# Feed-forward input products as seven products of quarters, with the inner features in slabs

## The chip, the cores and the metric

One core of one Trainium2 chip runs the whole program in one launch. The metric is device microseconds of an execution. A core has a matrix engine (TensorE, "PE" in the profile) whose weight loads are listed apart ("PEld"), and VectorE (DVE), ScalarE (ACT) and GpSimd (POOL), each of which works through its own instructions in program order. SyncE (SP) issues most DMAs. Matmuls write to PSUM, which here is used as two pairs of banks and four single banks.

## The reference, cut to what matters

Two layers act on 528 tokens (16 learned ones ahead of 512) of 1024 features, in float32. Each has a feed-forward block, a token mixer (layer 0 differential attention, layer 1 gated linear attention) and a second feed-forward block:

```python
def rmsnorm(x, g):
    y = x * lax.rsqrt(jnp.mean(x * x, axis=-1, keepdims=True) + RMS_EPS)
    return y * g

def swiglu(h, w_in, w_out):            # w_in 1024 x 5632, w_out 2816 x 1024
    gu = h @ w_in
    g, u = gu[..., :D_FF], gu[..., D_FF:]
    return (jax.nn.silu(g) * u) @ w_out

for i in range(2):
    h = h + 0.5 * swiglu(rmsnorm(h, ffn1_norm[i]), ffn1_w_in[i], ffn1_w_out[i])
    h = h + mixer_i(rmsnorm(h, mix_norm[i]))
    h = h + 0.5 * swiglu(rmsnorm(h, ffn2_norm[i]), ffn2_w_in[i], ffn2_w_out[i])
return rmsnorm(h, final_norm)[:, 16:]
```

The four feed-forward blocks are called a, b (layer 0) and c, d (layer 1) here and in tile names: `ps_bi` is PSUM of b's input products, `ps_bo` of its output products. Block d needs only the last 512 tokens.

## The kernel before, in words

The residual `xr` lies in SBUF, features on partitions, as eight tiles of 128 x 528. Each float32 product is done in three passes over two exact parts of each operand, high (`h`) and low (`l`): wh*xh, wh*xl, wl*xh (`linear`, L230). ScalarE casts the high part of a chunk of weights (`split_chunk`, L190), VectorE or GpSimd subtracts it for the low part (L191); a chunk is 128 x 1024 and there are three rooms for chunks (raw, high and low). Chunks come in one list (`plan`) in order of use, and each `take` loads and splits those behind it.

The norm's gain goes into the activations' parts (`split_x`, L283 on ScalarE, L284 on VectorE); 1/rms (`rms_scale`) multiplies what comes out. It comes from a sum of squares that GpSimd adds up tile by tile (`add_square`, L296 and L300), a product with ones (L339) and a chain on ScalarE and VectorE (L305 to L312).

A feed-forward block (`ffn`) first runs 44 input products, g and u for each of 22 inner features of 128 rows. Each takes eight blocks of the contraction, three passes, two halves of the tokens of 264 columns into two banks (in d one pass of 512 columns into one bank). `done` scales by 1/rms, applies silu and multiplies (L457 to L466); the parts of all 22 hidden features stay in SBUF. Then `project_out` runs eight output products of 22 blocks each; behind each, VectorE adds to the residual (L369) and the parts and the square for the next norm are made. The next stage starts on seven eighths of its first contraction before it needs the last block. At the very start three products run side by side while pieces of x and of the weights come in. `finish` does the last output block by halves of the tokens, so that one half's final norm runs under the other half's matmuls.

Everything is in program order (`manual_schedule`); the mixers place their steps by slots and ranks (`timeline`), with projections as filler, and the first three blocks of their output products begin under the last head (`finish_all`).

## Time and profile before

| | |
|---|---|
| median of 3 runs | 2118.15 us (2115.76 to 2120.3) |
| span of the profiled execution (its own time is given by this) | 2114.5 us |
| TensorE matmuls busy | 2062.8 us, 98% |
| VectorE, ScalarE, GpSimd busy | 1080.8, 739.8, 259.1 us |
| input products of b, without its first contraction | 743.78 to 993.34 us |
| output products of b | 993.34 to 1120.64 us |
| HBM read | 174.26 MB, 83 GB/s |

Times are counted from the first instruction. Matmuls are pipelined, so the duration of one (285 ns for 264 columns) is longer than the distance from one start to the next. The chain of waits is followed back from the last instruction to what released each step.

### The profile page before, as it was taken

To read this page: it belongs to the slowest core of one execution; us is meant where nothing else is said; L and a number is where in the kernel's file an instruction comes from. 1 tells how busy PE (TensorE), PEld (TensorE's weight loads), DVE (VectorE), ACT (ScalarE), POOL (GpSimd) and SP (SyncE) were. 2 spreads that over 40 slices of the span, in tenths; PEclk is the share of its full clock that TensorE was granted. 3 is DMA by queue.
4 is the path that set the end of the run, shared out by engine and by line. 5 is a ranking of instruction groups with operands and counts; after the bars stand their busy time and mean duration, and the time that the engine had idled before them with its cause. 6 is when DMAs were issued, how large, how long until landed. Compare 5 with 4: busy or idle time off the path is not lost.

```text
span 2114.5 us, 34232 instructions
## 1 busy us (share of the span) xinstructions
PE 2062.8 (98%) x14654; PEld 1920.3 (91%) x14654; DVE 1080.8 (51%) x1653; ACT 739.8 (35%) x1224; POOL 259.1 (12%) x193
## 2 busy tenths in 40 slices
PE   8999999999899999999999999999999999999998
PEld 8999999977777999999999999999988878888886
DVE  6444433488888654444334444433366665444333
ACT  5222222355555432222223222222544452222223
POOL 2000000334331200000000000000333220000001
PEclk9999999999999999999999999999999999999999
DMA  4233233211110223233322223233222222332332
GB/s 156 96 90 91 88 93 90 81 51 40 42 49 31 81 90 91 90 91 95 90 86 97 95 90 91 88 93 90 81 71 70 71 90 90 100 96 94 92 97 71
DMA packets 52586, 178.57 MB, mean 84 GB/s; under 512 B 5825, under 2 KB 8002, under 8 KB 52434
## 3 DMA queue, kind: packets, MB, share of 16 engines
q1 hardware_dynamic: 52112, 176.25, 27.2%
q8 instruction: 115, 1.88, 0.4%
q14 instruction: 37, 0.30, 0.0%
q10 hardware_dynamic: 322, 0.13, 0.0%
HBM read 174.26 MB, written 2.10 MB: 83 GB/s over the span
## 4 chain that ended last, share of the span: by engine, by line
PE 88%; DVE 8%; ACT 2%; issue 1%; DMA 0%; POOL 0%; SPq 0%; DVEq 0%; ACTq 0%; POOLq 0%
PE ps_bi L230 12%; PE ps_ci L230 12%; PE ps_ai L230 12%; PE ps_di L230 11%; PE ps_co L230 6%; PE ps_ao L230 6%; PE ps_bo L230 6%; PE ps_do L230 5%; PE ps_dak L230 2%; PE ps_dao L230 2%; PE ps_glao L230 2%; PE ps_gva L230 1%; PE ps_s L642 1%; PE ps_gvb L230 1%; PE ps_gob L230 1%
## 5 line engine op out<-in xcount | busy, mean ns | idle before, releaser
L230 PE MATMUL ps_ai<-xh,wh_ai 128*128 128x264 f32 x704 | 144.2, 286 | 5.4 <-ACT xh L283 5.3
L230 PE MATMUL ps_ai<-xl,wh_ai 128*128 128x264 f32 x704 | 143.0, 284 | 1.1 <-DVE xl L284 1.0
L230 PE MATMUL ps_ci<-xh,wh_ci 128*128 128x264 f32 x704 | 143.1, 285 | 0.0
L230 PE MATMUL ps_bi<-xh,wh_bi 128*128 128x264 f32 x704 | 143.1, 285 | 0.0
L230 PE MATMUL ps_ai<-xh,wl_ai 128*128 128x264 f32 x704 | 142.1, 284 | 0.5 <-DVE wl_ai L191 0.5
L230 PE MATMUL ps_bi<-xl,wh_bi 128*128 128x264 f32 x704 | 141.9, 283 | 0.0
L230 PE MATMUL ps_ci<-xl,wh_ci 128*128 128x264 f32 x704 | 141.9, 283 | 0.0
L230 PE MATMUL ps_bi<-xh,wl_bi 128*128 128x264 f32 x704 | 141.3, 282 | 0.0
L230 PE MATMUL ps_ci<-xh,wl_ci 128*128 128x264 f32 x704 | 141.3, 282 | 0.0
L230 PE MATMUL ps_di<-xh,wl_di 128*128 128x512 f32 x352 | 138.8, 394 | 0.0
L230 PE MATMUL ps_di<-xh,wh_di 128*128 128x512 f32 x352 | 138.7, 394 | 0.0
L230 PE MATMUL ps_di<-xl,wh_di 128*128 128x512 f32 x352 | 137.3, 390 | 0.0
L230 PEld LDWEIGHTS ps_ai<-xh,wh_ai 128*128 128x128 f32 x704 | 109.3, 189 | 5.8 <-ACT xh L283 5.3
L230 PEld LDWEIGHTS ps_ai<-xl,wh_ai 128*128 128x128 f32 x704 | 109.9, 189 | 1.8 <-DVE xl L284 1.8
L230 PEld LDWEIGHTS ps_ai<-xh,wl_ai 128*128 128x128 f32 x704 | 108.7, 188 | 1.0 <-DVE wl_ai L191 1.0
L230 PEld LDWEIGHTS ps_ci<-xl,wh_ci 128*128 128x128 f32 x704 | 109.2, 188 | 0.0
L230 PEld LDWEIGHTS ps_bi<-xl,wh_bi 128*128 128x128 f32 x704 | 109.2, 188 | 0.0
L230 PEld LDWEIGHTS ps_ci<-xh,wh_ci 128*128 128x128 f32 x704 | 108.7, 188 | 0.1
L230 PEld LDWEIGHTS ps_bi<-xh,wh_bi 128*128 128x128 f32 x704 | 108.7, 188 | 0.1
L230 PEld LDWEIGHTS ps_bi<-xh,wl_bi 128*128 128x128 f32 x704 | 108.2, 188 | 0.0
L230 PEld LDWEIGHTS ps_ci<-xh,wl_ci 128*128 128x128 f32 x704 | 108.2, 188 | 0.0
L673 ACT ACTIVATE e<-ps_s,nb,rq 64x264 f32<-64x264 f32 (+3 forms) x96 | 54.6, 570 | 83.6 <-DVE nb L662 53.9
(544 smaller groups left out, 5199.3 us busy)
## 6 DMA issues: line engine op xcount, KB each, us to landing
wraw_bi<-in_f_in SPq DMA_DIRECT2D x44, 512.0 KB, 3.6
wraw_ci<-in_f_in SPq DMA_DIRECT2D x44, 512.0 KB, 3.6
wraw_di<-in_f_in SPq DMA_DIRECT2D x44, 512.0 KB, 3.6
wraw_ai<-in_f_in SPq DMA_DIRECT2D x41, 512.0 KB, 3.6
wraw_ao<-in_f_out SPq DMA_DIRECT2D x16, 512.0 KB, 3.6
wraw_bo<-in_f_out SPq DMA_DIRECT2D x16, 512.0 KB, 3.5
wraw_co<-in_f_out SPq DMA_DIRECT2D x16, 512.0 KB, 3.5
wraw_do<-in_f_out SPq DMA_DIRECT2D x16, 512.0 KB, 3.5
```

Source lines behind the costliest of these rows:

```text
L230: nc.tensor.matmul(put(b, at, at + c1 - c0), w[:, ws], x[:, c0:c1], start=first, stop=last,)
L642: nc.tensor.matmul(o, qm[m][rows, qs], kl[rows, c0 : c0 + n], start=False, stop=True)
L673: act.activation(es_[t][m][: NQ[t], c0:c1], p, AF.Exp, bias=nb, scale=rq[: NQ[t], t : t + 1], accum_out=sm[:, i, m : m + 1],)
```

## The change

Write the 256 rows of g and u of an inner feature as two block rows, the contraction as two halves (even and odd tiles of 128 features) and the tokens as two halves. The product of a 2 x 2 and a 2 x 2 of quarters takes eight products of quarters; Strassen's method (in a form with shared sums) takes seven, P1 to P7, of sums and differences of quarters. P1 uses A11 and the first half of even x, P2 uses A12 and the first half of odd x; the others use s1 to s4 (weights, four sums a feature, on VectorE) and t1 to t4 (activations, four differences of each pair of tiles). The sums of the seven products go partly through PSUM: P1, P6, P5 and P3 add up in one bank, P7 and P4 in another, and what lies between is copied or added out (`evacuate`).

The seven products have 4 blocks of the contraction, three passes and one half of the tokens each. Inner features are taken in slabs of 2, 4, 4, 4, 4, 4; while the input products of a slab run, the output products of the slab before are put between them, each block of a slab adding to the residual by itself. Output weights come in pieces of up to 512 columns. The last slab's output products stand alone at the end of the block, with the sums for the next norm behind each. All stages share two SBUF areas (`ra`, `fa`) by fixed offsets. The loading order at the start changes, and the squares of x are now behind all sums (`head`).

Core of the diff (new code; the old `ffn`, `want_ffn` and `next_parts` go):

```diff
+SLABS = (2, 4, 4, 4, 4, 4)
+NQ = KD // 2
+AHEAD = 6
+NRING = 9
+    def plain(i, gcol, tok, k):
...
+        act.activation(h, x, AF.Copy, scale=g)
+        dve.scalar_tensor_tensor(l, x, g, h.bitcast(F32), op0=ALU.mult, op1=ALU.subtract)
+    def scaled(i, gcol, tok, k, z):
...
+        act.activation(z[:, 2 * k : 2 * k + 2, :n], tokens(xr[j], tok), AF.Copy, scale=...)
+        if k == 0:
+            dve.tensor_tensor(out=z[:, 4, :n], in0=z[:, 0, :n], in1=z[:, 1, :n], op=ALU.subtract)
+    def sums(i, tok, z, fine):          # t2, t3, t4 on DVE, then parts of t1..t4
...
+            out(3, 7)                   # act.copy of 4 x 264
+            rest(3, 7)                  # dve subtract of 4 x 264
+    def next_block(kind, gcol, acc, j, c0, z=None, last=False):
+        if kind == "parts":
+            split_x(j, gcol, c0)
+        elif kind == "seven":
+            plain(i, gcol, tok, k)
+        add_square(acc, j, c0)
+        if kind == "seven":
+            scaled(i, gcol, tok, k, z)
+            if k:
+                sums(i, tok, z, last and j == KD - 1)
...
+    def in_units():
+        order = [(0, "P1"), (1, "P1"), (0, "P2")]
+        order += [(0, p) for p in ("P6", "P7", "P5", "P3", "P4")] + [(1, "P2")]
+        for f in range(1, KF):
+            order += [(f, p) for p in ("P6", "P7", "P5")]
+            order += [(f + 1, "P1"), (f, "P3"), (f, "P4"), (f + 1, "P2")]
...
+    class in_stream:                    # tasks in order: s1, s2, s3, cut P6, s4, cut P7, ...
+        def step(self):                 # a sum on DVE, or a cast on ACT and a subtract on DVE
...
+            def evacuate(f, p):
+                if p == "P1":
+                    act.copy(g[:, 0], A)
+                elif p == "P2":
+                    dve.tensor_tensor(out=g[:, 0], in0=banks["B", f], in1=g[:, 0], op=ALU.add)
+                    if R:
+                        dve.tensor_tensor(out=g[:, 0], in0=g[:, 0], in1=r(0), op=ALU.mult)
+                elif p == "P6":
+                    act.copy(u[:, 0], A)
+                elif p == "P5":
+                    act.copy(u[:, 1], A)
+                    dve.tensor_tensor(out=u[:, 1], in0=banks["D", f], in1=u[:, 1], op=ALU.add)
+                elif p == "P3":
+                    dve.tensor_tensor(out=g[:, 1], in0=A, in1=r(1), op=ALU.mult)
...
+                    act.activation(g, g, AF.Silu)
+                elif p == "P4":
+                    dve.tensor_tensor(out=u[:, 0], in0=banks["D", f], in1=u[:, 0], op=ALU.add)
+                    dve.scalar_tensor_tensor(u, u, -1.0, r(), op0=ALU.mult, op1=ALU.mult)
...                                      # later: u *= g, its high part (ACT), its low part (DVE)
+            def product(f, p):
...
+                for i in range(NQ):
+                    for c, (w, v) in enumerate(((wh, xh), (wh, xl), (wl, xh))):
+                        nc.tensor.matmul(banks[k, f], w[:, ws], v, ...)
+            def bring(c, what):         # output weights: load, or cast, subtract and load c + 2
...
+            for i, u in enumerate(work):
+                if len(u) == 3:
+                    out_piece(*u)
+                else:
+                    product(*u)
...                                      # stream.step() up to AHEAD products on; late steps
+                    evacuate(*u)
+                    if u == (0, "P6"):
+                        R.append(rms_scale(acc, name, c0))
...
+            for j in range(KD):         # the last slab's output products
+                for c in range(pieces(tail)):
+                    out_piece(tail, j, c)      # piece 0 also brings the next weights
...
+                out_done(tail, j)              # add to the residual; next_block
+                if kind == "parts" and j in (5, 6):
+                    split_to(j - 5)
+                if kind == "seven" and j >= 4:
+                    nxt.to(2 * (j - 3))
...
+            if z == 0:                  # in finish, now over the last slab alone
+                table(LN_EXP)
...
+                if j == 5:              # behind the mixers' output blocks
+                    ahead.start()
+                    ahead.to(2)
+            ahead.to(6)
...
+    load_x(0, 2)
+    first.load(0, 0)
+    load_x(4, 6)
+    first.load(1, 0)
+    load_x(1, 3, 5, 7)
+    first.load(0, 1)
+    first.load(1, 1)
+    def head(z):
+        for i in range(KD // 2):
+            plain(i, V_F1[0], False, 0)
+            if i in (0, 3):
+                first.to(1 + i // 3)
+        for i in range(KD // 2):
+            plain(i, V_F1[0], False, 1)
+        first.to(3)
+        zs = [z, room_for_sums(fa[:, ZF : ZF + 8 * HALF])]
+        for i in range(KD // 2):
+            for k in range(2):
+                scaled(i, V_F1[0], False, k, zs[i % 2])
+            sums(i, False, zs[i % 2], False)
+        first.to(6)
+        for k in range(KD):
+            add_square(acc, k)
```

## Rows read from the trace of the kernel before

**Rows 1.** The page: busy time of each engine, and the granted clock in slices.
```profile
PE 2062.8 (98%) x14654; PEld 1920.3 (91%) x14654; DVE 1080.8 (51%) x1653; ACT 739.8 (35%) x1224; POOL 259.1 (12%) x193
...
PEclk9999999999999999999999999999999999999999
```
**Rows 2.** Chain that ended last: start us, us, engine, tile, line, count.
```profile
64.17 202.73 PE ps_ai L230 x1680
...
742.89 0.89 PE ps_ss_b L339 x4
743.78 249.55 PE ps_bi L230 x2070
993.34 127.31 PE ps_bo L230 x1056
...
1741.84 238.06 PE ps_di L230 x1035
...
2086.15 7.85 PE ps_last L402 x66
```
**Rows 3.** Window over the input products of b (columns: header line).
```profile
core 0: us, PE busy (x) PEld busy (x) DVE busy (x) ACT busy (x) POOL busy (x), PEclk, DMA share, GB/s
743.78:993.34 249.56, 249.56 (x2073) 249.56 (x2072) 116.09 (x136) 70.53 (x91) 0.00 (x0) 1.00 0.30 92
```
**Rows 4.** Timeline of TensorE: 272 columns, one bank (start us, us).
```profile
695.34 0.29 PE L740 MATMUL ps_o<-aTh,vh 128*128 128x272 f32 x1
...
695.98 0.29 PE L740 MATMUL ps_o<-aTh,vl 128*128 128x272 f32 x1
```
**Rows 5.** Groups by line: a weight load of b (busy us, mean ns).
```profile
L230 PEld LDWEIGHTS ps_bi<-xl,wh_bi 128*128 128x128 f32 x704 | 109.2, 188 | 0.0
```
**Rows 6.** Timeline of VectorE, 23 to 33 us.
```profile
23.74 0.43 DVE L311 SCALAR_TENSOR_TENSOR nT_a<-nT_a,nA_a 128x264 f32<-128x264 f32 x1
24.21 0.43 DVE L312 SCALAR_TENSOR_TENSOR R_a<-nT_a,R_a 128x264 f32<-128x264 f32 x1
24.56 0.43 DVE L310 TENSOR_TENSOR nT_a<-R_a 128x264 f32<-128x264 f32 x1
...
31.51 0.71 DVE L466 TENSOR_TENSOR hla<-tua,hha 128x528 fp32r<-128x528 f32 x1 [0.77 <-ACT hha L465]
32.14 1.22 DVE L191 TENSOR_TENSOR wl_ai<-wraw_ai,wh_ai 128x1024 fp32r<-128x1024 f32 x1
```
**Rows 7.** Timeline of ScalarE at the start.
```profile
8.11 0.60 ACT L190 CAST wh_ai<-wraw_ai 128x512 fp32r<-128x512 f32 x1
8.62 0.73 ACT L283 ACTIVATE xh<-xr,vec 128x528 fp32r<-128x528 f32 x1
9.26 0.63 ACT L296 ACTIVATE sq<-xr 128x528 f32<-128x528 f32 x1
9.79 0.60 ACT L190 CAST wh_ai<-wraw_ai 128x512 fp32r<-128x512 f32 x1
```
**Rows 8.** Timeline where the attention's heads end.
```profile
707.78 1.22 DVE L191 TENSOR_TENSOR wl_dao<-wraw_dao,wh_dao 128x1024 fp32r<-128x1024 f32 x1
...
709.06 0.51 PE L230 MATMUL ps_dao<-oh,wl_dao 128*128 128x264 f32 x2 [1.57 <-DVE wl_dao L191]
```
**Rows 9.** DMA, 0 to 40 us in 40 slices; POOL's additions of squares.
```profile
GB/s 0 37 243 359 229 280 406 403 385 338 400 407 260 23 94 356 74 0 111 332 98 78 246 201 0 0 0 0 0 0 102 311 111 0 131 279 180 213 225 37
...
L300 POOL TENSOR_TENSOR acc_in<-acc_in,sq 128x528 f32<-128x528 f32 x7 | 10.5, 1498 | 8.1 <-ACT sq L296 8.0
```
**Rows 10.** Timeline of VectorE at the end: the first half's multiplications.
```profile
2098.08 2.85 DVE L423 TENSOR_TENSOR xr<-xr,R_fin 128x256 f32<-128x256 f32 x5
2100.86 0.47 DVE L418 SCALAR_TENSOR_TENSOR xr<-xr,vec,R_fin 128x256 f32<-128x256 f32 x1
```
**Rows 11.** Timeline of TensorE: a wait in the attention.
```profile
411.79 0.38 PE L919 MATMUL ps_rq<-ones,row 1*128 1x1 f32 x2 [1.20 <-DVE row L915]
```
**Rows 12.** The window right behind that wait (columns as in rows 3).
```profile
412.00:414.00 2.00, 2.00 (x12) 1.99 (x12) 1.17 (x2) 1.48 (x2) 0.00 (x0) 0.65 0.61 154
```

More of the change, by code (lines that the diff above doesn't have):

```diff
@@ L142, in hybrid_trunk_kernel, with parts_at, begin @@
     pool.memset(epst, EPS)
+    ra = xpool.tile([P, RA], F32R, tag="ra", name="ra")
+    fa = xpool.tile([P, FA], F32, tag="fa", name="fa")
+    def parts_at(c, n):
+        return ra[:, c : c + n], ra[:, c + n : c + 2 * n]
     plan = []
-    raws, parts_of = [], []
     taken = [0]
     reach = [0]
+    loaded, asked, cast = [0], [0], [0]
+    low, used = [], []
+    def begin():
+        for x in (plan, low, used):
+            x.clear()
+        for x in (taken, loaded, asked, cast):
+            x[0] = 0
     def want(src, nk, name, eng=None):
@@ L254, in finish_all @@
         for i, b in enumerate(blocks):
-            load_to(taken[0] + i)
             patient[0] = True
+            run(b)
+            after = list(later)
+            later.clear()
             split_to(taken[0] + i)
             patient[0] = False
-            run(b)
             flush()
+            for f in after:
+                f()
     def timeline(events, filler, rate):
@@ L336, in rms_scale @@
         pss = []
+        ps = pair(f"ps_ss_{name}")
         for h in range(2):
-            p = bank(f"ps_ss_{name}{h}")[:, :hn]
+            p = ps[:, h, :hn]
             nc.tensor.matmul(
@@ new lines, in scaled, with out, rest @@
+    def scaled(i, gcol, tok, k, z):
+        j = 2 * i + k
+        n = SEQ // 2 if tok else HALF
+        act.activation(
+            z[:, 2 * k : 2 * k + 2, :n], tokens(xr[j], tok), AF.Copy,
+            scale=vec[:, gcol + j : gcol + j + 1],
+        )
+        if k == 0:
+            dve.tensor_tensor(
+                out=z[:, 4, :n], in0=z[:, 0, :n], in1=z[:, 1, :n], op=ALU.subtract
+            )
+    def sums(i, tok, z, fine):
+        n = SEQ // 2 if tok else HALF
+        h, l = [t[:, :, :n] for t in seven(i)]
+        b12, b21, b22, t1, t3, t2, t4 = [z[:, c, :n] for c in range(1, 8)]
+        def out(a, b):
+            act.copy(h[:, a:b], z[:, a + 1 : b + 1, :n])
+        def rest(a, b):
+            dve.tensor_tensor(
+                out=l[:, a:b], in0=z[:, a + 1 : b + 1, :n], in1=h[:, a:b].bitcast(F32),
+                op=ALU.subtract,
+            )
+        if fine:
+            out(3, 4)
+        dve.scalar_tensor_tensor(t2, b22, -1.0, t1, op0=ALU.mult, op1=ALU.subtract)
+        if fine:
+            out(5, 6)
+        dve.tensor_tensor(out=t3, in0=b22, in1=b12, op=ALU.subtract)
+        if fine:
+            out(4, 5)
+            rest(5, 6)
+        dve.scalar_tensor_tensor(t4, t2, -1.0, b21, op0=ALU.mult, op1=ALU.subtract)
+        if fine:
+            out(6, 7)
+            rest(4, 5)
+            rest(3, 4)
+            rest(6, 7)
+        else:
+            out(3, 7)
+            rest(3, 7)
@@ L350, in new_acc, with all_parts @@
+    def all_parts():
+        return [parts_at(2 * L * k, L) for k in range(KD)]
     def new_acc(name):
@@ L378, in finish, with stream_slot @@
+    def stream_slot(u):
+        f, p = u
+        return f - 1 if p in ("P1", "P2") and f > 0 else f
+    def finish(acc, ws_, hidden, slab):
         j = KD - 1
         n = SEQ // 2
-        g = [vec[:, V_FIN + k : V_FIN + k + 1] for k in range(KD)]
+        g = vec[:, V_FIN + j : V_FIN + j + 1]
+        wh, wl = ws_
         ps = pair("ps_last")
-        chunks = []
         y = npool.tile([P, L], F32, tag="R", name="R_fin")
@@ L999, in gla @@
             act.dma_start(raw2, gla_g2)
-            w2 = early("Sl", F32R, "w2")
+            Shs, Sls = [[part(2 * DV) for _ in range(2)] for _ in range(2)]
+            w2 = Sls[0]
             pool.memset(w2.bitcast(F32), 0.0)
@@ L1317, in gla @@
             split_to(taken[0] + 1)
[L1318 removed]
+            for j, b in enumerate(blocks[3:], 3):
                 run(b)
[L1320 to L1334 removed]
```

551 lines of the change are left out of this document (378 added, 173 removed).

## The prediction

> **What bounds the kernel now.** I read the page's totals first, then the chain that ended last, then the stretches one by one. The totals [rows 1] show TensorE busy for 2062.8 of 2114.5 us, VectorE for 1080.8, ScalarE for 739.8, and the granted clock at its upper level in every slice. The chain [rows 2] says what that busy time is: in the input products of a feed-forward block it is one unbroken run of matmuls (2070 in 249.55 us), with no releaser from another engine between them; the 1056 matmuls of the output products behind it are the same. The windows [rows 3] confirm it: TensorE 249.56 of 249.56 us, VectorE 116 us, ScalarE 71 us. So inside the four feed-forward blocks only fewer or shorter matmuls help, and every wait that the change adds to TensorE's queue is a plain loss. Unit prices from [rows 2]: a matmul of 264 columns 249.55/2070 = 0.1206 us, of 512 columns 238.06/1035 = 0.2300 us, of 256 columns 7.85/66 = 0.1189 us.
>
> **What the change removes.** For each of 22 inner features and each of blocks a, b, c, before: 2 x 8 x 3 x 2 = 96 matmuls of 264 columns, 96 x 0.1206 = 11.57 us. After: 7 products x 4 x 3 = 84. They all add up in one bank, as the 256- and 512-column ones do now; the line through those two (7.8 ns + 0.434 ns a column) gives 0.1224 us at 264 columns. The bounds are 0.1206 (what 264 columns cost now, in two banks by turns) and 0.128 (272 columns in one bank, 0.64 us over five starts [rows 4]); I take 0.1224, the fit of the longest runs. 84 x 0.1224 = 10.28 us, a gain of 1.29 a feature, 28.4 a block, 85.3 for three (93 to 54). Block d: before 48 x 0.2300 = 11.04, after 84 matmuls of 256 columns at 0.1189 = 9.99, gain 23.1 in all. Together **-108.5 us**. The output products keep their 1056 matmuls.
>
> In [rows 5] a weight load is shown with 188 ns, yet loads and matmuls alternate every 0.12 us in [rows 2], so the load hides. The Trainium skill (TensorE: Matmul & The Clock Gate, Back-to-back issue gap) speaks against block d: pairs of load and matmul sustain about 81 ns at 128 columns and 131 at 512, so short matmuls are dear. Interpolated, an estimate from that page, 256 columns would cost 98 ns and d would go from 1056 x 0.131 = 138 to 1848 x 0.098 = 181 us, 42 slower instead of 23 faster. The trace disagrees with both of its prices (0.2300 and 0.1189), so the rows decide.
>
> **What it adds in the steady loop.** VectorE gets more work and must not become the bound. Start to start [rows 6], 264 elements take 0.35 us (24.21 to 24.56), 0.47 if the operation needs the one just before it (23.74 to 24.21), 528 take 0.63 (31.51 to 32.14); between them 512 cost 0.61 and 1056 about 1.2. Per feature: 4 weight sums and 7 low parts of 512, 6.8; five evacuations of 264 columns, two of them dependent, 2.0; scale, product and low part of u over 528, 2.0; and, as 48 output chunks fall on 22 features (2.18 each, because slabs of four add to the residual six times instead of once), 2.18 x (0.63 + 0.61) = 2.7. Sum 13.5 us, against 84 x 0.1224 + 48 x 0.1206 = 16.07 us of TensorE. ScalarE needs about 7 us: 0.51 for a cast of 512, 0.53 to square and 0.64 to scale 528 [rows 7]. The cuts of weights run six products (8.8 us) ahead and the evacuations have at least one product of slack; the worst burst, three sums and a cut (2.5 us), hides beneath that. The loads gain no bytes: output weights come as 48 pieces of 256 KB where 24 chunks came, each behind a low part on VectorE and asked for two pieces ahead, on queues that are 0.30 busy [rows 3]. I book **+5 us** for slab changes; the bounds are 0 and, if VectorE's waits for ScalarE come on top (about 3 us a feature), 45.
>
> **What it adds where stages meet.** Before, a join costs almost nothing, since an output block lasts 132 matmuls (15.9 us) and the next product has 42 matmuls before it needs the last block. Now the last slab has 24 matmuls (2.9 us) a block, and behind each block stand the sums of the activations, in strict order on two engines. From [rows 6, 7], an even block: evacuation 0.7, first parts and square and scaled copy on ScalarE to 2.4, difference 0.45, then the output weights' low part 0.6: 3.6 us. An odd block: evacuation 0.7, parts, square, copy 1.9, three sums 1.2, a cast of 1056 1.1, its low part 1.2, weights 0.6: 6.8 us. A pair is 10.4 us where TensorE has 5.8.
> - *b to c*: three pairs and the even block, 34.8, with 6.6 of sums and cuts for block c between (queued behind them on VectorE), bring TensorE's last output block to an end at about 41.5 us instead of 23.2: +18. Then VectorE is some 13 us behind, and product P4 of feature 0 may not write its bank before VectorE's add after P5 has read it; behind the sums stand three weight sums, 1/rms (eight operations of 264, 3.2) and two cuts: +8. **+26** (14 to 34).
> - *attention to b*: [rows 8] already show the first block behind the heads waiting 1.57 us for VectorE. The eight blocks' sums (about 37 us of VectorE and its waits, plus cuts of 1.2) fit the 30 us of matmuls behind them only just: +3.5. Then P1, P1 (2.9 us) cover the join, but the cut of P2 stands behind the last sums (8 us), P6 behind three weight sums (10.6), P4 behind 1/rms (22.6 where TensorE alone would be there at 11): +11.5. **+15**; *gated attention to d* the same with 256 columns, **+14** (7 to 20 each).
> - *a to attention, c to gated attention*: evacuation 0.7, parts 0.7 + 0.7, weights 0.6 and a wait for their cast, 3.2 us a block against 2.9, and two casts for the next stage: **+4 each** (0 to 8).
> - *the start*: now the first block, whose input products end at 64.17 + 202.73 = 266.90, loses 266.90 - 2112 x 0.1206 - 0.89 (the norm's matmuls) = 11.4 us [rows 2]. After, P1, P1, P2 run as x comes in; at the loading rate of [rows 9] (about 0.3 to 0.4 MB a us from 2 us on) x is there at 12 us. Then ScalarE and VectorE make four groups of sums in turn, 3.9 us each (scaled 1.3, differences 1.3, cast 1.05, waits), to 29 us; the cuts of P6, P7, P5 end at 33; only then come eight squares on ScalarE, and POOL's seven additions at 1.35 to 1.5 us [rows 9] behind the second of them end at 44. 1/rms stands in TensorE's queue right behind P6, so P7 starts at about 45. With 48 matmuls (5.9 us) and the norm's (0.9) done by then the loss is 38, or 27 more than now, and P4 waits 1.5 beyond: **+28** (20 to 34).
> - *the end*: the last block's halves shrink from 66 matmuls to 12, so the first half's multiplications, 3.2 us on VectorE [rows 10], no longer hide beneath the second half's matmuls, and the square sum of block 6 (POOL) is late for the first: **+4** (1 to 7).
>
> Sum: -108.5 + 5 + 26 + 15 + 14 + 8 + 28 + 4 = **-8.5 us**. On the profiled span 2114.5 becomes 2106. The median of the runs, 2118.15, is 3.65 above that span (the profiled execution's time is given by its span alone; what lies around it I leave as it is), so I predict 2110. A difference of under 0.2% (2113.9 to 2122.4) can't be told from none.
>
> **Rivals.**
> 1. *The joins cost half.* The chains assume that ScalarE and VectorE never overlap in a block; where the casts of one block run beneath the sums of the other, and the first cuts of the next stage lie ahead, b to c, the two attention joins and the tails (63) fall to 25 or so: 2110 - 42 = 2068. For it: in [rows 6] VectorE starts the next operation 0.08 us before the last ends, and ScalarE 0.1 us before [rows 7]. Against it: program order puts each low part right behind the cast that it needs.
> 2. *VectorE becomes the bound of the loop (the other side).* From 16.07 us a feature on, each 0.1 us costs 8.8 us. At 13.5 of work, 3.1 of waits (four low parts straight behind their casts, two evacuations that wait for ScalarE) decide; half a microsecond beyond gives 2110 + 40 = 2150, slower. For it: 84% is near, and the low parts of the output weights follow their casts at once. Against it: ScalarE has half its time free, so casts are early whenever VectorE is late.
> 3. *The clock falls in the joins.* After a wait of 1.20 us for VectorE [rows 11] the granted clock of the next two microseconds is 0.65 [rows 12], between the levels of 1.2 and 2.4 GHz. Five joins with matmuls and waits by turns would pay some 12 us of half-speed matmuls (b's tail 5, the restarts 1.5 each): 2122, no change. The Trainium skill (TensorE: Matmul & The Clock Gate, Why this matters for your kernels) has that idle stretches between bursts bring the lower clock back; the row agrees.
> 4. *One bank costs 0.128 a matmul*, as the 272 columns show: 5544 x 5.6 ns = 31 us, 2141. Against it: those have other shapes among them.
>
> **How the numbers follow.** Forecast 0.46 (2094 to 2122: faster 0.30, same 0.14, slower 0.02), rival 1 0.24 (faster), rival 2 0.20 (slower), rival 3 0.06 (half same, half slower), rival 4 0.04 (slower). Faster 0.54, same 0.17, slower 0.29. The range runs from rival 1's time to rival 4's: below 2068 lie the cheaper half of rival 1 (0.12), above 2142 some 0.1 of rival 2.
>
> **What would show it.** Right: input matmuls at 0.119 to 0.124 us start to start; TensorE idle for some 38 of its first 45 us, POOL's additions releasing the last wait, and for 18 of the last 41 us of b, VectorE releasing; hardly any idle in the features between. Wrong: VectorE at 95% in the loop with TensorE released by low parts (rival 2); joins under 10 us (rival 1); a start that loses under 20 us.

## The result, and the profile after

The changed kernel takes 2156.55 us (median of 4, 2153.21 to 2158.8) against 2118.1 (4 runs, 2115.76 to 2120.3): ratio 1.0185, 95% interval 1.017 to 1.0199. The profiled span grew from 2114.5 to 2156.4 us, by 41.9, where 8.5 less were forecast.

The page after: busy time, the granted clock in slices (compare [rows 1]), and the chain that ended last by engine.

```profile
PE 1998.1 (93%) x14600; PEld 1876.3 (87%) x14600; DVE 1706.7 (79%) x3138; ACT 1037.9 (48%) x2077; POOL 259.0 (12%) x193
...
PEclk7999999999999999999998999999999998999998
...
PE 67%; DVE 21%; ACT 8%; issue 3%; DMA 0%; POOL 0%; SPq 0%; DVEq 0%; ACTq 0%
```

The same chain line on the page before:

```profile
PE 88%; DVE 8%; ACT 2%; issue 1%; DMA 0%; POOL 0%; SPq 0%; DVEq 0%; ACTq 0%; POOLq 0%
```

This pair of lines holds the result. The chain passes through TensorE for 0.67 x 2156 = 1445 us in place of 1861. What left it is more than the matmuls that were saved (119 us, counted below): long pieces of the chain now run through VectorE (169 to 453 us), ScalarE (42 to 173) and issue (1% to 3%, time for which the profile shows no wait). Where, the windows show: the first 120 us, one slab of a's loop, the first 100 us of b, c and d (their restarts), and between the first two of these the end of b (its tail).

```profile
core 0: us, PE busy (x) PEld busy (x) DVE busy (x) ACT busy (x) POOL busy (x), PEclk, DMA share, GB/s
0.00:120.00 120.00, 77.67 (x573) 74.76 (x574) 92.14 (x170) 66.67 (x121) 10.42 (x15) 0.87 0.31 100
183.11:247.36 64.25, 64.25 (x531) 64.13 (x530) 53.62 (x93) 28.85 (x57) 0.00 (x0) 1.00 0.32 100
...
762.10:862.00 99.90, 87.47 (x675) 85.03 (x674) 91.39 (x167) 53.23 (x108) 2.62 (x2) 0.97 0.30 93
1108.50:1156.60 48.10, 33.56 (x216) 31.98 (x215) 34.30 (x51) 23.07 (x38) 7.91 (x6) 0.82 0.23 77
1156.60:1256.00 99.40, 90.03 (x709) 87.89 (x708) 90.19 (x168) 53.80 (x110) 1.78 (x2) 0.98 0.32 99
...
1771.60:1871.00 99.40, 86.30 (x629) 81.49 (x628) 91.52 (x169) 54.11 (x111) 2.56 (x2) 0.93 0.30 93
```

The loop is as forecast: 64.25 us for four features, 16.06 each (16.07 forecast), TensorE busy throughout, VectorE 53.62/4 = 13.4 (13.5 forecast). The restarts are not: VectorE is busy for 0.91 to 0.92 of their 100 us, and TensorE for only 0.87 to 0.91. In b's tail 216 matmuls at 0.1206 would take 26 of 48 us. TensorE's timeline at the end of b and the start of c (start us, us, releaser of the idle time in brackets):

```profile
1151.93 1.69 PE L738 MATMUL ps_bo<-ra 128*128 128x264 f32 x6 [7.16 <-ACT ra L719]
1153.42 3.32 PE L738 MATMUL ps_bo<-hidb,ra 128*128 128x264 f32 x18
1156.58 3.09 PE L692 MATMUL ps_cA<-ra 128*128 128x264 f32 x24
1159.50 1.63 PE L692 MATMUL ps_cB<-ra 128*128 128x264 f32 x12
1164.69 2.12 PE L692 MATMUL ps_cA<-ra 128*128 128x264 f32 x12 [3.55 <-ACT ftc L646]
...
1174.03 1.73 PE L692 MATMUL ps_cA<-ra 128*128 128x264 f32 x12 [2.21 <-ACT ftc L654]
1176.76 1.72 PE L692 MATMUL ps_cD<-ra 128*128 128x264 f32 x12 [1.00 <-DVE ftc L655]
```

The last output block of b waits 7.16 us for ScalarE's cast of its weights (L719). In c, P6 of feature 0 waits for ScalarE's copy of P1 (L646), since both use bank A, P3 for the copy of P5 (L654), P4 for VectorE's sum (L655). ScalarE's own timeline says why the copies are late:

```profile
1163.23 1.13 ACT L573 CAST ra<-fa 128x512 fp32r<-128x512 f32 x2
1164.27 0.65 ACT L646 COPY ftc<-ps_cA 128x264 f32<-128x264 f32 x2
...
1167.86 0.62 ACT L573 CAST ra<-fa 128x512 fp32r<-128x512 f32 x1 [2.43 <-DVE fa L586]
...
1168.78 1.28 ACT L369 ACT_TABLE_LOAD   x1
...
1172.06 1.64 ACT L573 CAST ra<-fa 128x512 fp32r<-128x512 f32 x3
1173.60 0.37 ACT L654 COPY ftc<-ps_cA 128x264 f32<-128x264 f32 x1
```

P5's copy of 0.37 us (L654) stands behind a cast of weights that waits for VectorE's sums of weights (2.43), the table load, 1/rms and three more casts. At the start of a the wait for P1's copy is the largest of the run; below it, what stands ahead of that copy on ScalarE:

```profile
43.90 3.01 PE L692 MATMUL ps_aA<-ra 128*128 128x264 f32 x12 [27.53 <-ACT fta L646]
```

```profile
41.90 0.64 ACT L339 ACTIVATE sq<-xr 128x528 f32<-128x528 f32 x1 [0.73 <-POOL acc_in L343]
42.45 1.12 ACT L573 CAST ra<-fa 128x512 fp32r<-128x512 f32 x2
43.48 0.37 ACT L646 COPY fta<-ps_aA 128x264 f32<-128x264 f32 x1
```

**Where the 41.9 us are.** For every stretch I took the distance from each matmul to the next, less the price of its shape in [rows 2] (0.1206, 0.1189, 0.2300 us); the sum is what the stretch loses. "Start" is a block's first 100 us, "tail" its last 45; attention and GLA (the two mixers) are from their first matmul to that of the next block.

```
                         forecast   measured (after - before)
matmuls and loop         -108.5 + 5   -119.2 + 8.5 (0.1217 for 0.1206 us)
start of a                 +28        +39.5  (lost 43.3, 6.4 before; begins 2.6 later)
tail of a                   +4         +8.7
attention, start of b      +15        +23.7  (5.3 + 18.8 - 0.4)
tail of b, start of c      +26        +36.1  (22.3 + 14.2 - 0.4)
tail of c                   +4         +9.9
GLA, start of d            +14        +24.7  (5.6 + 19.5 - 0.4)
tail of d, end              +4         +9.4
sum                        -8.5       +41.3
```

The gain came, and the loop has hardly a wait: its 8.5 us are the price of a matmul, 0.1217 in the mean where the count takes 0.1206. Each of the seven places where stages meet cost 1.4 to 2.5 times its forecast: 152 us for 95.

### The profile page after: what moved, and what is told of

The parts are those of the page before. It is cut to its first block, busy times and chain, and to the rows that moved or that the text cites. A ratio compares the mean times of both kernels' runs of the same rounds, so it can differ in the third digit from the quotient of the medians.

```text
span 2156.4 us, 36646 instructions
## 1 busy us (share of the span) xinstructions
PE 1998.1 (93%) x14600; PEld 1876.3 (87%) x14600; DVE 1706.7 (79%) x3138; ACT 1037.9 (48%) x2077; POOL 259.0 (12%) x193
## 4 chain that ended last, share of the span: by engine, by line
PE 67%; DVE 21%; ACT 8%; issue 3%; DMA 0%; POOL 0%; SPq 0%; DVEq 0%; ACTq 0%
PE ps_aA L692 5%; PE ps_ao L738 5%; PE ps_co L738 5%; PE ps_bo L738 5%; PE ps_bA L692 5%; PE ps_cA L692 5%; PE ps_do L738 4%; PE ps_dA L692 4%; DVE ra L598 3%; PE ps_aD L692 3%; PE ps_bD L692 3%; PE ps_cD L692 2%; PE ps_dak L269 2%; DVE fa L586 2%; PE ps_dD L692 2%
## 5 line engine op out<-in xcount | busy, mean ns | idle before, releaser
L573 ACT CAST ra<-fa 128x512 fp32r<-128x512 f32 x616 | 367.9, 619 | 193.2 <-DVE fa L586 190.0
L598 DVE TENSOR_TENSOR ra<-fa,ra 128x512 fp32r<-128x512 f32 x616 | 416.9, 687 | 17.0 <-ACT ra L573 10.8
L586 DVE TENSOR_TENSOR fa<-fa 128x512 f32<-128x512 f32 x352 | 235.7, 686 | 3.1
L720 DVE TENSOR_TENSOR ra<-fa,ra 128x512 fp32r<-128x512 f32 (+1 forms) x192 | 134.0, 700 | 85.5 <-ACT ra L719 84.6
L692 PE MATMUL ps_aA<-ra 128*128 128x264 f32 x1056 | 143.7, 289 | 39.6 <-ACT fta L646 27.5
L692 PEld LDWEIGHTS ps_aA<-ra 128*128 128x128 f32 x1056 | 135.8, 192 | 41.4 <-ACT fta L646 27.7
L692 PE MATMUL ps_cA<-ra 128*128 128x264 f32 x1056 | 140.6, 285 | 7.5 <-ACT ftc L654 4.0
L692 PE MATMUL ps_bA<-ra 128*128 128x264 f32 x1056 | 140.6, 285 | 6.0 <-ACT ftb L654 3.7
L692 PE MATMUL ps_dA<-ra 128*128 128x256 f32 x1056 | 138.2, 283 | 6.5 <-ACT ftd L654 3.7
L692 PEld LDWEIGHTS ps_dA<-ra 128*128 128x128 f32 x1056 | 133.4, 190 | 11.6 <-ACT ftd L654 5.5
L719 ACT CAST ra<-fa 128x512 fp32r<-128x512 f32 (+1 forms) x192 | 111.0, 580 | 0.5
L738 PE MATMUL ps_bo<-ra 128*128 128x264 f32 x432 | 63.6, 292 | 15.4 <-ACT ra L719 14.4
```

The costliest lines, as they stand in the source:

```text
L573: act.copy(self.parts(n)[0], self.raw(f, OF[self.order[n][1]]))
L586: dve.tensor_tensor(out=self.raw(f, x), in0=self.raw(f, a), in1=self.raw(f, b), op=ALU.add)
L598: dve.tensor_tensor(out=l, in0=self.raw(f, q), in1=h.bitcast(F32), op=ALU.subtract)
L692: nc.tensor.matmul(banks[k, f], w[:, ws], v, start=(p in ("P1", "P2", "P7") and i == 0 and c == 0), stop=(i == NQ - 1 and c == 2), skip_gr ...
L719: act.copy(h, raw)
L720: dve.tensor_tensor(out=l, in0=raw, in1=h.bitcast(F32), op=ALU.subtract)
```

## The experiments

Losses of all kernels, by that count (us), and medians; the loop, d's tail and the end are not in the table. The kernel before, run again beside each group of runs, had medians of 2116.6 to 2120.1, so differences of 3 us between rows mean nothing.

The expectations name theories by letters. J: the activations' sums make the joins long. C: copies out of the banks stand behind casts of weights. K: the lower clock. W: the casts of output weights in the tails. B: VectorE's busy time alone. D: the path runs through ScalarE and VectorE by turns. P: POOL and VectorE slow each other.

```
                  a start tail  b start tail  c start tail  d start  att.  GLA    median
after               43.3   8.7   18.8   22.3   14.2   9.9   19.5   348.9  238.3  2156.6
no_sums             28.9   9.1   15.8   10.8   10.8   7.8   14.9   341.5  233.8  2108.6
sq_pool             44.3   6.0   21.4   23.4   15.2   6.1   19.8   350.7  245.2  2167.5
copies_first        48.5   9.9   23.3   22.3   17.9  10.1   22.1   345.1  238.3  2179.5
three_rooms         44.7   2.9   21.0   11.9   24.0   2.8   21.0   352.2  245.5  2155.7
no_low01            41.3   9.2   16.3   21.9   11.7   8.7   15.0   347.9  238.8  2143.4
late_R              44.6   9.9   21.9   22.4   14.5   7.9   20.4   345.1  236.7  2159.9
adds_dve            43.1   5.6   19.2   21.5   12.8   7.1   20.4   345.1  235.0  2144.4
lag                 45.4   7.9   21.4   22.5   14.5   9.9   21.1   350.2  237.1  2161.5
no_R                40.0   7.9   17.6   23.9   10.0   7.9   18.0   349.1  238.3  2144.8
ahead4              46.0   9.4   25.5   23.3   16.5   9.2   22.7   346.2  238.2  2168.0
combo1              42.6   5.4   18.8   24.0   14.8   5.4   19.5   349.4  237.8  2151.7
combo2              43.1   0.8   21.0   11.8   24.5   0.8   19.6   351.1  242.7  2146.4
long_tail           43.4   5.3   18.8   16.4   13.3   3.8   21.6   346.2  235.3  2146.5
long_adds           43.3   3.4   20.8   16.9   12.9   3.4   20.6   344.9  234.9  2139.8
warm                39.0   7.9   16.0   14.3    9.5   9.4   16.7   350.3  236.4  2159.0
long_rooms          44.7   2.3   18.9    6.5   22.3   2.3   21.5   348.3  235.8  2140.0
long_rooms_adds     43.6   2.3   19.2    5.8   20.8   2.3   20.1   344.5  236.6  2133.5
best_ahead7         46.0   2.3   22.7    5.4   24.9   2.3   23.9   343.1  236.7  2174.8
```

### What work costs: no_sums, no_low01, no_R

```diff
-        if kind == "seven":
-            scaled(i, gcol, tok, k, z)
-            if k:
-                sums(i, tok, z, last and j == KD - 1)
-    X_OF = {"P1": 0, "P2": 1, "P3": 2, "P5": 3, "P7": 4, "P6": 5, "P4": 6}
+    X_OF = {"P1": 0, "P2": 1, "P3": 2, "P5": 1, "P7": 2, "P6": 1, "P4": 2}
```

(and the groups of sums in `head`.)

> Leaves out the sums of the activations everywhere (products P6, P7, P5, P4 are fed with the plain quarters), so the output is not the reference's; all 84 matmuls a feature, all casts and low parts of weights, all copies out of the banks stay. In the changed kernel TensorE loses, against the kernel before, some 39 us at the start of a, 18 at the start of b, 22 in b's tail, 14 at the start of c, 19 at the start of d, 9 and 10 in the tails of a and c. Theory J (the joins are long because the sums stand in ScalarE's and VectorE's queues): the start gives back 18, b's tail 12, the starts of b, c and d 7 to 12 each; 2156 falls by 50 to 70, to 2086 to 2106. Rival C (the copies of P1 and P5 out of the banks stand behind casts of weights that wait for VectorE, whatever the sums do): the starts of b, c, d keep at least 12 us each, 2156 falls by under 30. Rival K (TensorE's clock at its lower level in the joins): nothing but what the shorter idle stretches give, under 15.

2108.6, 48 less: just short of J's span, beyond the totals of C and K. By place it is mixed: the start of a gave 14.4, b's tail 11.5, the mixers 7.4 and 4.5, but the starts of b, c and d only 3.0 to 4.6, where J asked for 7 to 12; they keep 15.8, 10.8 and 14.9, in two of three cases as C has it. The sums are a third of what the joins cost; the rest stays, for instance P3 of c's feature 0, whose bank is copied out (L650 here) behind 1/rms:

```profile
1132.51 1.72 PE L688 MATMUL ps_cA<-ra 128*128 128x264 f32 x12 [3.49 <-ACT ftc L650]
```

```diff
-            dve.tensor_tensor(out=l, in0=self.raw(f, q), in1=h.bitcast(F32), op=ALU.subtract)
+            if f > 1:
+                dve.tensor_tensor(out=l, in0=self.raw(f, q), in1=h.bitcast(F32), op=ALU.subtract)
```

> Leaves out VectorE's subtraction for the low part of the input weights in the first two features of each block (their matmuls run with the high part a second time, so the output is not the reference's); 14 operations of 512 elements a block, 14 x 0.61 = 8.5 us of VectorE, everything else stays. Theory B (a restart lasts until VectorE has worked off what is queued: it is 0.87 to 0.88 busy in the first 33 to 38 us of b, c and d, and in the first slab no output products lie between, so a feature has 10.3 us of matmuls for about 10.8 of VectorE): the starts of b, c, d (18.8, 14.2, 19.5 us lost) give back 6 to 9 each, a's 4 to 8, the tails of b and before b and d a little: 2156 becomes 2119 to 2133. Rival C (the order on ScalarE, P5's copy behind the 1/rms chain, sets it): under 8 us in all, 2148 or more.

2143.4, 13 less: between the two, with 2.0, 2.5, 2.5 and 4.5 us at the starts of a to d for 8.5 us of VectorE work each. VectorE's busy time alone is not the bound.

```diff
-                        R.append(rms_scale(acc, name, c0))
+                        y = npool.tile([P, L], F32, tag="R", name=f"R_{name}")
+                        pool.memset(y, 0.25)
+                        R.append(y)
```

> Leaves out 1/rms in the four feed-forward blocks: a constant takes its place, the norm's matmuls, two loads of ScalarE's table, Ln, Exp and eight operations of VectorE (3.4 us) in each block are gone, so the output is not the reference's. Theory D (from the middle of a tail to the end of the next first slab the path runs through ScalarE and VectorE by turns, TensorE only fills it): in c's restart the 1/rms chain stands on that path from 1168.78 to 1174.55 us, 5.8 us, of which 2 are VectorE waiting for ScalarE; without it the starts of a, b, c, d give back 4 to 6 each: 2156 becomes 2132 to 2141. Rival B (only VectorE's busy time counts): 1.5 to 3 each, as the leaving out of 8.5 us of low parts gave 2.5 to 4.5: 2144 to 2150. If the chain lies beside the path: within 4.

2144.8, 12 less, 1.2 to 4.2 a start: rival B's span, less than D. In both runs a start gives back less than the length of the work that is gone; no single piece of work is the whole path.

### What order costs: copies_first, late_R, lag, ahead4, three_rooms

```diff
                     product(*u)
+                    evacuate(*u)
                 between = 1
...
-                    evacuate(*u)
```

> Behind each product its evacuation (ScalarE's copies and VectorE's sums out of the banks) is issued ahead of the next cuts of weights, not behind them. Rival C: the waits of P6, P3 and P4 of the first features for ScalarE's copies go, 8 to 15 us over four blocks: 2141 to 2148. Theory J: the copies of the first feature stand behind the sums, not behind the weights' casts, so under 4 us are gained; and as the cuts now stand behind evacuations that wait for TensorE, the loop, at 13.5 of 16.07 us on VectorE, may lose 0 to 10: 2152 to 2166.

2179.5, 23 more: a miss for both. Each start loses 2.6 to 5.2 us more. In c, P3's wait for its copy falls from 2.21 to 1.07 us, as C has it, but the cast of the first output weights, issued behind the evacuations, comes late instead. TensorE in the changed kernel, then in this one:

```profile
1201.59 2.12 PE L738 MATMUL ps_co<-ra 128*128 128x264 f32 x12 [0.73 <-ACT ra L719]
```

```profile
1212.90 3.01 PE L738 MATMUL ps_co<-ra 128*128 128x264 f32 x12 [3.64 <-ACT ra L719]
```

```diff
-                    if u == (0, "P6"):
+                    if u == (0, "P5"):
                         R.append(rms_scale(acc, name, c0))
```

> The norm's matmul and the 1/rms chain are issued behind P5's evacuation of feature 0, not behind P6's. Rival C: P3(0) no longer waits for P5's copy behind the 1/rms chain and three casts on ScalarE (2.2 us in c, 1.9 in a), and P4(0)'s 1.0 goes too; 2.5 to 3.5 us back at each of the four starts: 2142 to 2148. Theory B: VectorE has the same work in another order, so the waits come back at P2(1) or P3(1): within 4 us of 2156.

2159.9, as B has it. P3 of feature 0 no longer waits, but P5 of feature 1 does, for the copy of P6 (L652), now behind the late chain:

```profile
1183.64 6.20 PE L692 MATMUL ps_cA<-ra 128*128 128x264 f32 x36 [2.47 <-ACT ftc L652]
```

```diff
-            rest(3, 7)
+            lagging.append(lambda: rest(3, 7))
...
```

(`...`: each is issued behind the next block's plain parts.)

> The low part of each group of activation sums is issued one block later (at the start one group later), so that VectorE no longer stands still for ScalarE's cast of 1056 elements (1.14 us a group). Theory B: VectorE's idle time in the chains of sums goes, 3 x 1.1 us at the start, at both attention joins and in b's tail, partly to waits elsewhere: 8 to 13 us back, 2143 to 2148. Rival W (in the tails the cast of the next output weights behind the activations sets the time): start 3, joins 1 each: 2150 to 2153.

2161.5, a miss for both: taking away the 1.14 us a group for which VectorE stood still gave nothing back.

```diff
-AHEAD = 6
+AHEAD = 4
```

> Weights are cut four products ahead in place of six. Theory D: in a restart two cuts and up to three weight sums fewer stand ahead of the first evacuations on VectorE and ScalarE, and the loop, where VectorE has 15% of its time free, takes them on: 1 to 3 us back at each start, 2146 to 2153. Rival (the cover of six products is needed in the loop, since sums, cut and evacuations of a feature come in a burst): waits of TensorE in every feature, 2160 or more.

2168.0, the rival's side, though not by waits in the loop: the first 100 us of b, c, d lose 2 to 7 us more. Four products of cover are too few there.

```diff
-                    bring(c + 1, 1)
+                    if c <= len(chunks) - KD:
+                        bring(c + 1, 1)
+                    if c >= len(chunks) - KD:
+                        bring(c + 2, 1)
...
```

(`...`: the third room lies in the ring of input weights.)

> In the last slab the output weights have three rooms in place of two, and each block's weights are cast and cut two blocks ahead, before the block in front is evacuated. Rival W (the tails are long because each block's weights are cast behind the activations of the block before): of 8.7, 22.3, 9.9 and 2.9 us lost in the tails of a, b, c, d half goes, 2156 becomes 2134 to 2142. Theory J: the tails of a and c, where a block needs 3.2 us on both engines in turn, give back 5 us each, b's, where a pair needs 10.4 us of chain for 5.8 of matmuls, 3 at most: 2156 becomes 2141 to 2150.

2155.7, nothing, though W was right on the tails: those of a, b and c lose 23 us less. It all comes back (c's start 9.8, GLA 7.2, attention 3.3, the other starts 5), and c's first product now waits for x itself:

```profile
1153.73 3.98 PE L692 MATMUL ps_cA<-ra 128*128 128x264 f32 x15 [5.87 <-ACT ra L411]
```

Of five changes of order none gained by itself: three stay within 5 us of the changed kernel and two are slower. That fits a path that runs through ScalarE and VectorE by turns, where a wait that goes at one place comes back at the next. With a longer last slab the same third room did gain (long_rooms, below).

### Squares, POOL and the start: sq_pool, adds_dve, combo1, combo2

```diff
     def head(z):
+        for k in (0, 2, 4, 6, 1, 3, 5, 7):
+            add_square(acc, k, eng=pool)
```

(The eight squares behind the sums go; `next_block` passes POOL too.)

> The squares of the residual go from ScalarE to POOL, at the start as x comes in (ahead of all sums) and in every join. Theory J: at the start POOL's chain of eight squares and seven additions ends at about 32 us in place of 45, and TensorE is then bound by the cuts of P6, P7, P5 and by 1/rms: 8 to 12 us back; in b's tail ScalarE is relieved of 0.53 us a block, 3 to 4 back; 1 to 3 at each other join: 2156 becomes 2132 to 2142. Rival (the sums' own chain is the later one everywhere, the squares lie beside it): under 5 us in all. Rival C: under 5 us too, since P1's copy stands behind casts all the same. If POOL, at 2.6 us a block against 2.9 of TensorE, ends later than ScalarE did, the norm's matmul in b, c, d comes later and the time rises by up to 8.

2167.5, 11 more. POOL was done at 25.9 us, not 45, and P6 still came at 45.7. VectorE's timeline of the changed kernel, then of this one, while POOL works beside it:

```profile
11.31 2.91 DVE L412 SCALAR_TENSOR_TENSOR ra<-xr,vec,ra 128x528 fp32r<-128x528 f32 x4
```

```profile
14.12 6.52 DVE L412 SCALAR_TENSOR_TENSOR ra<-xr,vec,ra 128x528 fp32r<-128x528 f32 x4
```

The same four operations take 2.2 times as long: what POOL took over from ScalarE, VectorE paid for.

```diff
-            pool.tensor_tensor(out=acc[:, c0:], in0=acc[:, c0:], in1=sq[:, c0:], op=ALU.add)
+        def add():
+            (adder or pool).tensor_tensor(
...
+        add_square(acc, j, c0, adder=dve if kind else None, wait=adds if kind else None)
```

(in all joins but the last; in `head` two squares follow each group of sums.)

> The seven additions of squares go from POOL to VectorE, in all joins but the last, and at the start the squares are made between the groups of sums, not behind them. Theory P (POOL and VectorE slow each other: low parts of 528 elements took 6.52/4 = 1.63 us while POOL squared and added, against 2.91/4 = 0.73 without): an addition of 0.63 on VectorE replaces one of 1.36 to 1.66 on POOL that costs VectorE about 1 us, so the joins get 1 to 3 us shorter each, and a's start, where POOL's last addition ends at 45 us, gives back 6 to 10: 2156 becomes 2132 to 2146. Rival (no contention, VectorE's backlog only grows): the start gives back 6 to 8, each of five joins loses 3 to 4.4: 2160 to 2172.

2144.4, 12 less, at the upper end of P's span, and not where P had most of it: a's start still loses 43.1. The joins, tails and mixers gave it (attention 3.8, GLA 3.3, a's and c's tails 3 each).

```diff
+            scaled(i, gcol, tok, k, z)
             plain(i, gcol, tok, k)
...
-            scaled(i, gcol, tok, k, z)
```

(beside the edits of adds_dve.)

> The additions of squares on VectorE as in the run before (2144), and in the joins of b, c and d the scaled copy on ScalarE goes ahead of the plain parts and the square, so that the differences on VectorE start 1.0 us earlier in each block. Theory D: the square (0.53) and the plain cast (0.51 to 0.65) leave the path between an output block and the sums behind it; 0.5 us in each of 8 blocks of three joins, less what comes back elsewhere: 2132 to 2141. Rival (the low parts of the plain halves, now behind the differences, are late instead): 2142 to 2148.

2151.7: 7 more than adds_dve, a miss for both, on the rival's side. It is lost mostly in attention (+4.3), GLA (+2.8) and b's tail (+2.5). The rival's reason (late low parts of the plain halves) was not traced.

> The run combo1 with the three rooms for output weights in the last slab. Alone the rooms shortened the tails by 24 us (a 5.8, b 10.4, c 7.1, d 1.6) and all of it came back at the next start (attention 3.3, c 9.8, GLA 7.2, b and d 4). Theory D: what bounds a join is the work of ScalarE and VectorE by turns, and the rooms do not shorten it: within 5 us of combo1. Rival W (with VectorE relieved, the weights' casts are the next bound): 6 to 14 us below combo1.

The edits of combo1 and three_rooms together. 2146.4, 5.3 below combo1, between the two and next to D's bound of 5: the tails lose 21 less, the starts of b and c and the mixers take back 18.

### The clock and the cover: warm, long_tail, long_adds, long_rooms, long_rooms_adds, best_ahead7

```diff
+                    if f"{u[0]}{u[1]}" in ("0P6", "0P3"):
+                        keep_busy(pair(f"ps_w{name}{u[1]}")[:, 0, :HALF], 24 if u[1] == "P6" else 12)
...
+                if kind == "seven" and j in (1, 3, 5):
+                    keep_busy(bank(f"ps_w{name}{j}")[:, :HALF], 24)
```

> TensorE is given matmuls that nobody reads where it stands still: 24 behind output blocks 1, 3, 5 of b's last slab, 24 ahead of P6 and 12 ahead of P3 of feature 0 in each block (at the upper level 2.9 and 1.5 us, where it waited 3.2 to 7.2, 3.6 and 2.2). Rival K (the lower clock level in the joins is on the path): matmul time at the lower level in the joins falls from some 19 us to under 10 and the time by 5 to 14: 2142 to 2151. Theory D (the path runs through ScalarE and VectorE, slow matmuls lie beside it): the records show fewer slow matmuls, the time stays within 4 of 2156, or rises by up to 10 where the added matmuls are themselves in the way.

2159.0. Windows over the last 44 us of b, of the changed kernel and of this one (columns as above):

```profile
1113.00:1156.60 43.60, 29.06 (x179) 27.48 (x178) 30.53 (x45) 21.91 (x36) 7.91 (x6) 0.80 0.24 79
```

```profile
1116.00:1159.80 43.80, 34.74 (x247) 33.70 (x246) 30.89 (x46) 21.92 (x36) 7.97 (x6) 0.88 0.25 79
```

The granted clock rose from 0.80 to 0.88, and b as a whole took 396.7 us for 394.5. In the table the added matmuls count as work; with 4.3 us a start and 8.7 in b's tail put back, warm equals the changed kernel within 2 everywhere. Theory D's side: in b's tail the lower level was there and was not paid for, so far as one kernel with matmuls added can show it. The test is a partial one: over the first 38 us of d the clock rose too (0.82 to 0.91), over those of b (0.91) and c (0.95) it stayed.

```diff
-SLABS = (2, 4, 4, 4, 4, 4)
+SLABS = (2, 4, 4, 4, 2, 6)
```

(with rooms of 768 for output weights and a ring of 8 for input weights.)

> Slabs of (2, 4, 4, 4, 2, 6) features in place of (2, 4, 4, 4, 4, 4), the rooms for output weights 768 wide, the ring of cut input weights 8 in place of 9: the last slab has 36 matmuls (4.34 us) a block in place of 24 (2.89), the number of matmuls in all is the same. Theory D (a join's loss is the time of ScalarE's and VectorE's chain less the matmuls beside it): the tails gain cover of 8 x 1.45 = 11.6 us each; b's loss of 22.3 falls to about 11, a's 8.7 and c's 9.9 to 0 to 2, d's 2.9 to 1, the starts keep theirs, the slab of two features costs 0 to 4: 2156 becomes 2124 to 2136. Rival (as with the three rooms, what the tail gives up comes back at the next start): 2150 to 2160.

2146.5, 10 less where D asked for 20 to 32. The places in the table gave back some 20 and d's tail 3; the loops of the four blocks lost 11 more (2 to 4 each), for a slab of two features that I had put at 0 to 4. Two of b's last blocks, from one wait to the next but one, of the changed kernel and of this one:

```profile
1123.87 0.76 PE L738 MATMUL ps_bo<-ra 128*128 128x264 f32 x4 [3.29 <-ACT ra L719]
...
1135.45 0.81 PE L738 MATMUL ps_bo<-ra 128*128 128x264 f32 x2 [3.23 <-ACT ra L719]
```

```profile
1114.20 0.76 PE L738 MATMUL ps_bo<-ra 128*128 128x264 f32 x4 [2.04 <-ACT ra L719]
...
1126.20 0.76 PE L738 MATMUL ps_bo<-ra 128*128 128x264 f32 x4 [2.09 <-ACT ra L719]
```

A pair takes 11.6 us with 5.8 us of matmuls in the changed kernel and 12.0 with 8.7 here: matmuls hardly enter into its length, and what is left is ScalarE's and VectorE's work. Ahead of the next runs I put the missing part down to matmuls that stand in a row with that work, since the weights of every second block are cast behind the activations.

> The run long_tail with the additions of squares on VectorE (alone 12 us below the changed kernel). Theory D, both add up: 2112 to 2124, level with the kernel before. Rival (the two take the same waits away): 2130 to 2145.

2139.8, in the rival's span: 7 below long_tail, where 12 would have been the sum.

> The run long_tail (2146) with three rooms for the cut output weights in the last slab, cast two blocks ahead. Theory D: the 36 matmuls of a block now lie beside the chain of about 11.5 us a pair, not in a row with it; b's tail and c's start together lose 22 to 25 in place of 30 (36 in the changed kernel), the tails of a and c nothing, of which 2 to 4 each come back in attention and GLA: 2132 to 2140. Rival (as alone, where 24 us came back in full): 2143 to 2150.

The edits of long_tail and three_rooms together. 2140.0, at the upper end of D's span, but not as D has it: tail of b and start of c lose 28.8 (29.7 without the rooms, 36.5 in the changed kernel) for 22 to 25 expected. So matmuls in a row with that work were not what was missing in b's join.

> The run long_rooms with the additions of squares on VectorE (12 us alone, 7 beside the longer slab). Theory D: 6 to 10 below long_rooms, 2124 to 2134; the start of a, 43 us lost against 11 in the kernel before, is not touched by any of this, so the kernel before (2118) stays ahead. Rival: no further gain, 2136 or more.

2133.5, in D's span; ratio 1.0062 (1.0047 to 1.0077) to the kernel before: 23 us of the 38 are back, the kernel before stays ahead. 43.6 us of a's start are untouched.

> The run long_rooms_adds with weights cut seven products ahead in place of six (four in place of six cost 11). If the first slab's waits come from cuts that are not far enough ahead: 3 to 6 below long_rooms_adds. Theory D (the cuts are VectorE work on the path wherever they stand): within 3.

2174.8, 41 more, a miss: with a ring of 8 a cast seven products ahead waits for its room (38 times in a, 40.6 us in all) and holds the copies behind it, now in the loop too, whose four stretches lose 31 us more. TensorE's wait for the copy of P6 in a (us, times, longest):

```profile
PE ps_aA L703 <- ACT fta L663: 13.0, 9, 2.6
```

## Why the prediction was wrong

- **Matmuls, right.** 16.06 us a feature for 16.07 forecast. With the slab's 192 output matmuls at 0.1206, the 336 of P1 to P7, in one bank, cost (64.25 - 23.16)/336 = 0.1223 where 0.1224 was taken, and block d's 256 columns came as [rows 2] had them. Rival 4 (0.128) is out.
- **Loop, right and better.** +5 us of waits forecast, next to none measured; VectorE 13.4 us a feature, 84%. Rival 2 (VectorE bounds the loop) is out as it was meant, since the loop has hardly a wait; that its 2150 lies nearest to the result is luck.
- **"What it adds where stages meet" failed**, in every term: 152 us for 95. I followed each join's chain to the one or two products that it holds first (P7 at the start; P2, P6 and P4 behind the attentions; P4 in c) and let TensorE run freely behind them. Those waits came: P2 of b and of d waits 4.9 and 5.1 us for the cast of its weights. Two things were missing behind them. First, the shared bank A puts ScalarE's copies between products: P6 and P3 of feature 0 wait for one, and so does P3 of the next features (0.61, 0.81 us in c). Second, I carried the loop's average into the first slab. There no output products lie between the input products: 84 x 0.122 = 10.25 us of matmuls for 13.4 - 2.7 = 10.7 of VectorE, so that slab wins nothing back. But no_low01 took 7 x 0.61 = 4.3 us a feature off VectorE just there and gave back only 2.0 to 4.5 us a start, so this ratio is a part of it at most.
- **What the runs show in its place**: the loss lies in the joins and not in the loop (the table); work of ScalarE and VectorE there is on the path, since leaving it out gives time back (48, 13, 12 us); that no change of order gained by itself speaks for a path through both engines and against one late instruction; and more matmuls beside that work (long_tail) gave some 20 us back at the joins. What the copies out of bank A cost by themselves is argued from the waits, not shown: no run gave P6 or P3 another bank.
- **The tails**, priced at 3.2 us a block against 2.9 for a and c and at 10.4 a pair for b, took 4.0 and 4.1 ((23.2 + 8.7)/8, (23.2 + 9.9)/8) and 11.6. The releaser named for b's was VectorE; it was mostly ScalarE, with the cast of the next output weights (the longest wait 7.16).
- **The start of a**: the chain of groups, cuts, squares and additions ran to 44.97 us as worked out (44 forecast), but P6 was to be done by then and only began at 43.9, behind the copy of P1; P7 began at 48.1 for 45. Of the 11.5 us missed, nearly 8 fall behind that, into the restart, for which only 1.5 had been booked. POOL's additions held not the norm's matmul, as forecast, but the copy of P1, through the squares that wait for them (0.73 in the rows above). They are no cause by themselves: with the additions on VectorE P6 comes at 42.6 (adds_dve), with POOL done at 25.9 at 45.7 (sq_pool), as the sums and cuts then end later.
- **Rival 3** (the clock falls, +12) saw the fall rightly, 0.80 to 0.82 in b's tail, and the price wrongly: in b's tail, where warm tested it, slow matmuls lay beside the path. **Rival 1** (half price) had the sign wrong.
- **Late loads**, which no run tests, are out as a cause: behind the first 10 us the profile names no DMA at the end of any wait of TensorE, VectorE, ScalarE or GpSimd.
- **Two side sums** are off, without weight in the forecast: at 0.1206 the gain of a, b and c would be about 95 us, not 93; and 63 falling to 25 makes rival 1 2072, not 2068.

What stays open: how the path divides between ScalarE and VectorE, as the pieces taken out gave back less than their length; what the rest of the 152 us is made of, as the leave-outs account for less than half and were not taken together; and whether a first slab that does the plain eight products until the sums are there would win, which was not tried.

## What to carry to other kernels

A change that takes work from the bound engine and gives it to idle ones is safe only in stretches where the idle ones run beside it; price each boundary up to the point where the backlog is worked off, with that stretch's own ratio of work, not with the loop's average. If a reordering removes a wait, look at the next stage's start before counting it: here 23 us left the tails and, with the short last slab, the whole of it came back there. Before trusting that an engine is free, check the copies out of a bank that the next matmul needs: in program order they stand behind whatever that engine was given before them, and behind what that waits for.

## What the runs showed of the hardware

POOL and VectorE slow each other: four operations of VectorE on 528 elements took 6.52 us beside POOL's squares and additions, 2.91 without, and moving the additions to VectorE gained 12 us although VectorE was the busier engine. Within sq_pool the difference of activations (L422) takes 1.54 us in the first group, while POOL works, and 0.43 in the second, behind POOL's end at 25.9 us:

```profile
22.03 1.54 DVE L422 TENSOR_TENSOR fta<-fta 128x264 f32<-128x264 f32 x1
...
28.89 0.43 DVE L422 TENSOR_TENSOR fa<-fa 128x264 f32<-128x264 f32 x1
```

POOL pays too: its square of 528 elements takes 1.07 us at 3.96 us, ahead of VectorE's work, and 1.52 at 13.60, beside it.

The Trainium skill (GPSIMD Engine Reference, Specifications) has that GpSimd shares its interfaces to SBUF with VectorE and that operations of VectorE with two inputs in SBUF contend. The operations here have two (`xr` and `ra`; in L422 two pieces of one tile), so the rows agree, and they give a price, which that table does not. Whether an operation with one input slows too was not looked at.
